# The recurrent layer's in-projections on pairs of float16 numbers, with block scales measured on the chip

## The chip, the cores and the metric

The kernel runs on one core of a Trainium2 chip. The metric is device time in microseconds of one execution. A TensorE matmul takes a stationary operand (the weights, which a separate load brings into the array) and a moving one; VectorE, ScalarE and GpSimd work beside it, each with its own instruction queue that is served in order.

## The reference

One step of a two-layer trunk on 512 prompt tokens and 32 sample tokens, 544 columns together, with a model width of 1024. Layer 0 is recurrent (RWKV-7), layer 1 is differential attention. Cut to what matters here:

```
h = rmsnorm(x, norm_w)
p, qm, gate = split(h @ w_in, [4736, 4736 + 512])     # w_in: 1024 x 7296 in layer 0
y_mix, S, last_row = rwkv_mixer(p, prev_row, S0, ...)  # token shift, then a scan over time
y_mem = mem_attention(qm, mk, mv)
x = x + (concat([y_mix, y_mem]) * silu(gate)) @ w_out
```

In the mixer each of p's columns is first blended with the column of the token before; then 24 heads of width 64 run `S = S * w + (S @ -kk) (kk * a) + v k`, and `y = S r`.

## The kernel before, in words

**Blocks.** Everything is kept transposed: features on the 128 partitions, tokens along the free dimension. A block of weights is 1024 x 128, eight tiles of 128 x 128. Layer 0's in-projection has 57 such blocks: 37 for p, 4 queries of the memory attention, 16 gates. For accuracy each fp32 operand is split into a high and a low part, and a product is three matmuls (high x high, high x low, low x high). The tokens are taken in two halves of 272. So a block is 2 x 8 x 3 = 48 matmuls of 128 x 272 into a PSUM bank (`steps`, line 481; for the first four blocks `gemm`, line 461).

**Two formats.** In layer 0 before the change the parts are fp32r. `load` (line 309) brings a block in two halves of 256 KB into the rotating tiles `raw`; `split` (line 425) queues, for each half, ScalarE's copy to the high part (`whi`) and VectorE's subtraction for the low part (`wlo`). In layer 1 the parts are float16, whose range is small, so each block is scaled by a power of two. `load_pair` (line 324) brings the block into one of four buffers inside the tile `h16s`; `square_total` (line 334) squares it with an accumulator on ScalarE, in two halves; `total_spread` (line 348) sums over the partitions by two matmuls of one column each with a matrix of ones; `scales` (line 364) makes from the sum, by integer arithmetic on the bits in VectorE, a power of two and its inverse; `scaled` (line 355) multiplies the block on GpSimd; `split_scaled` (line 393) makes the high and low parts, which the profile calls `whs`. The inverse scale enters where the product is read from PSUM. `scaled_pool` (line 1814) makes the buffers and constants for it between the layers.

**The recurrent chain.** The heads are taken in 12 pairs. For each pair `rw_chain` (line 1010) runs eight chunks of 64 tokens, one after the other, and a chunk (`chunk`, line 975) is a loop over engines: TensorE multiplies with the state (`ps_c<-SB,zr`), VectorE adds (`avz`), TensorE multiplies (`ps_c<-avz,at`), ScalarE copies (`sv`), TensorE multiplies (`ps_c<-sv,bt`), VectorE makes the new state (`SB`). Between two such hops TensorE works on the next pairs' preparation and on the in-projection blocks.

**The order of the work.** From line 1649 on every engine's order is fixed as written by the program. The loop over pairs (lines 1685 to 1724) calls the hops in turn; between them it takes work by a table (`PLAN`) and single in-projection matmuls from the generator `stream` (line 1609). How many matmuls go into a gap follows from due times, with a price per matmul, `MAIN`, in us. The blocks' jobs for ScalarE and VectorE (high parts, low parts, the shift's end) go into a queue, `put_off` (line 438). `some` (line 448) is called twice per hop and takes from its front: a job of price 0 (ScalarE's) at any call, one with a price (VectorE's) only if a budget for VectorE leaves room or the queue holds more than four jobs. `until` (line 443) forces out what a block needs, at its start. `stream` loads two blocks ahead and splits one ahead.

**Before that**, `inputs` (line 504) normalises and transposes the tokens and writes `hh` and `hl`, the two parts of h; the first four layer 0 blocks (36, 12, 0, 24) are projected outside the planned order, through `weights` and `used` (lines 404 and 413).

**Evacuations.** `shifted` (line 619) copies a p block from PSUM to `raw` on ScalarE and blends it; `gate_evac` (line 1056) makes the gate's tanh; `query_evac` scales the query.

Of the kernel before, what the change touches and what calls it, by code (L numbers as in the profile page):

```python
# [9 lines left out]
F32 = mybir.dt.float32  # L10
# [8 lines left out]
P = 128  # L19
D = 1024  # L20
KT = D // P
# [22 lines left out]
STAT1, SPREAD1, POWER1, SCALE1 = (14, 27), 12, 32, (37, 41)  # L44
SPLITS2, SCALE2 = (7, 11, 13, 17), (33, 36)
# [32 lines left out]
HOP, MAIN = 0.27, 0.126  # L78
# [64 lines left out]
class Trunk:  # L143
# [190 lines left out]
    def square_total(self, rec, q):  # L334

        if q == 0:
            rec["st"] = self.sts[rec["n"] % 4]
            if rec["n"] < 3:
                rec["junk"] = self.raws[3].bitcast(BF16)[:, :, :P]
            else:  # L340
                rec["junk"] = self.wp.tile([P, KT, P], BF16, tag="wlo", name="junkw", bufs=2)[:]
        k = slice(q * KT // 2, (q + 1) * KT // 2)
        with self.nc.allow_low_precision("a bound, rounded before a power of two is taken from it"):
            self.ae.activation(rec["junk"][:, k], rec["raw"][:, k], AF.Square, accum_out=rec["st"][:, q : q + 1])
# [37 lines left out]
    def measured(self, rec):  # L382

        if "s" not in rec:
            for q in range(2):
                self.square_total(rec, q)
            ps = self.psx.tile([P, 512], F32, tag="x", name="ps_st")
            self.total_spread(rec, ps[:, 0:1], True)
            self.scales(rec)
            for q in range(2):  # L390
                self.scaled(rec, q)

    def split_scaled(self, rec):
# [4 lines left out]
        ks = [slice(q * KT // 2, (q + 1) * KT // 2) for q in range(2)]  # L398
        todo = [(lambda k=k: self.ae.copy(hi[:, k], raw[:, k]), 0.0) for k in ks]
# [77 lines left out]
    def proj(self, src, c0, evac):  # L477
        self.gemm([self.weights(src, c0)], [(self.hh, self.hl)], evac)
        self.used()
# [24 lines left out]
    def inputs(self):  # L504

        nc, a = self.nc, self.a
        with ExitStack() as ctx:
# [16 lines left out]
            self.ahead = [(a["w_mem_k"][0], 3 * P)] + [(a["rw_in"][0], j * P) for j in (36, 12, 0, 24)]  # L524
# [10 lines left out]
            self.consts_norm(parB)  # L535
            ss = p.tile([P, 7], F32, name="ss")
# [60 lines left out]
            for k in range(KT):  # L597
                h = p.tile([P, TP], F32, tag="hn", name="hn", bufs=3)
                self.ve.scalar_tensor_tensor(h[:], xT[k], self.nw[0][:, k : k + 1], pr[0][:], ALU.mult, ALU.mult)
                self.ae.copy(self.hh[:, k, :TP], h[:])  # L600
                (self.ve if k in (2, 5, 7) else nc.gpsimd).tensor_tensor(self.hl[:, k, :TP], h[:], self.hh[:, k, :TP].bitcast(F32), ALU.subtract)  # L601
                if k in (3, 6):
                    next(kv)
                if k == 1:
                    sh = [P, KT, TS]
                    hs = p.tile(sh, F32, name="hs")
                    self.ve.tensor_tensor(hs[:], xs[:], self.nw[0].unsqueeze(2).to_broadcast(sh), ALU.mult)
                    self.ve.tensor_tensor(hs[:], hs[:], pr[1][:, :TS].unsqueeze(1).to_broadcast(sh), ALU.mult)
                    self.ae.copy(self.hh[:, :, TP:], hs[:])
                    self.ve.tensor_tensor(self.hl[:, :, TP:], hs[:], self.hh[:, :, TP:].bitcast(F32), ALU.subtract)  # L610
# [8 lines left out]
    def shifted(self, j, tag, bufs, w=None):  # L619
# [4 lines left out]
        made = {}  # L624

        def evac(ps, v):
            self.ae.copy(raw[:, v.start + 1 : v.stop + 1], ps)
            if w is not None and v.start:
# [18 lines left out]
        if w is None:  # L647
            self.proj(self.a["rw_in"][0], j * P, evac)
# [426 lines left out]
    def gate(self, src, c0, g):  # L1075

        sg, _, evac = self.gate_evac(self.o1[g])
        self.proj(src, c0, evac)
        return sg

# [8 lines left out]
    def rw_finish(self, st):  # L1089
# [31 lines left out]
        self.ve.scalar_tensor_tensor(sg[:], sg[:], 0.5, bv[:], ALU.mult, ALU.mult)  # L1121
# [63 lines left out]
    def mem_block(self, i, kind, h, mh, ml, w, out, ps_pool, ps_tag):  # L1185
# [4 lines left out]
        ps = self.psg.tile([P, 512], F32, tag="g", name="ps_g")  # L1190
        for k in range(KT):
            for u, x in ((0, mh), (0, ml), (1, mh)):
# [7 lines left out]
                yield  # L1200

# [13 lines left out]

    def mem_head(self, i, h, w, cq, cg, p):

        st = {}
        it = self.mem_steps(st, i, h, p)
        for _ in range(3):  # L1220
            next(it)
        st["q"], evac = self.query_evac(p)
        self.proj(w, cq + h * P, evac)
        for _ in range(9):
            next(it)
        sg = self.gate(w, cg + h * P, 12 + h)
        st["gate"] = lambda: sg
        for _ in it:
            pass
# [267 lines left out]
    def layer0(self, mem):  # L1497
# [6 lines left out]
        with ExitStack() as ctx:  # L1504
# [40 lines left out]
            def add(pr, src, c0, make):  # L1545
                blocks.append((src, c0, make))
# [3 lines left out]
            def add_gate(pr, st, c0, n):  # L1550
                def make(wt):
                    sg, st["gate"], evac = self.gate_evac(self.sg[n % SGB])
                    yield from self.steps(wt, evac)
                add(pr, w, c0, make)

            def add_shift(pr, of, q):
# [3 lines left out]
                add(pr, w, (12 * q + of) * P, make)  # L1560

            def add_query(pr, h):
                def make(wt):
                    mems[h]["q"], evac = self.query_evac(self.ma if h % 2 else self.rb2)
                    yield from self.steps(wt, evac)
                add(pr, w, RW_PROJ + h * P, make)
# [40 lines left out]
            blocks += [b + (None,) for b in after[:2]]  # L1607

            def stream():
                raws = [self.load(*b[:2]) for b in blocks[:2]]  # L1610
                wt = self.split(raws.pop(0))
                for _ in wt[1]:
                    self.put_off(*_)
                for i, (_, _, make) in enumerate(blocks):
                    wt, todo = wt
                    self.until(todo[-1][0])
                    if i + 2 < len(blocks):
                        raws.append(self.load(*blocks[i + 2][:2]))
                    nxt = self.split(raws.pop(0)) if raws else None
                    for _ in nxt[1] if nxt else ():  # L1620
                        self.put_off(*_)
                    if make is None:
                        self.made.append(wt)
                    else:
                        yield from make(wt)
# [117 lines left out]
        with ExitStack() as ctx:  # L1743
# [45 lines left out]
            self.scaled_pool()  # L1789
# [24 lines left out]
    def scaled_pool(self):  # L1814

        nc, p = self.nc, self.h0
        self.hh, self.hl = (lambda t: (t[:, 0], t[:, 1]))(p.tile([P, 2, KT, T], F16, tag="hl", name="h16"))
# [15 lines left out]
        with nc.allow_low_precision("a bound, rounded before a power of two is taken from it"):  # L1833
            self.ae.activation(sq, self.nw[1], AF.Square, accum_out=st)
# [4 lines left out]
        self.ve.tensor_scalar(self.nwx, self.nw[1], sx, None, ALU.mult)  # L1839
# [664 lines left out]
    def run(self):  # L2504
# [15 lines left out]
        self.hh = hp.tile([P, KT, T], F32R, tag="hh", name="hh")  # L2520
# [58 lines left out]
```

## Time and profile before

| what | value |
|---|---|
| runs before, median of 3 | 1345.06 us (1344.2 to 1348.67) |
| the profiled execution | 1347.07 us |
| its span, from the first to the last instruction | 1345.4 us |
| TensorE's granted clock, mean | 0.991 |
| layer 0's in-projection matmuls | 3 x 912, fp32r, from 35 to 698 us of the span |
| out-projection of layer 0 and what follows | 700 to 800 us |
| layer 1 | about 800 us to the end |

In the profile, PE is TensorE's matmuls, PEld its weight loads, DVE VectorE, ACT ScalarE, POOL GpSimd. A row names an operation by its tiles, `out<-in`, then the shape and type, how often it occurs (x), and after a bar the busy us in all and the mean ns of one; behind a second bar stands how long the engine was idle before these operations, and for whom it waited. Nearly all operations are issued through one helper, so they all have its line, L140, and are told apart by their tiles. In the lists of waits a row reads: who waited, for whom, us in total, times, the longest. Matmuls are pipelined, so their durations overlap; their pace is read from the starts.

### The profile page before, as it was taken

The numbers are of one execution on the slowest core, as the hardware profiler recorded it, in microseconds if no ns is written. First come the engines' busy times: TensorE is split into PE (matmuls) and PEld (weight loads), VectorE is DVE, ScalarE is ACT, GpSimd is POOL, SyncE is SP. The second block draws the span as 40 slices with busy tenths as digits, with TensorE's granted clock in tenths as the row PEclk, the third lists the DMA queues.
The fourth block names the chain that finished last, engine by engine and source line by source line (L and its number), as shares of the span: only waits on it lengthen the run. The fifth ranks groups of instructions, "written<-read, shape, count | busy, mean of one in ns | idle before, by whom it ended". The sixth has DMA issues, their size and how long they took to land. (4 is left out here: it accounts for less than half of the span.)

```text
span 1345.4 us, 32382 instructions
## 1 busy us (share of the span) xinstructions
PE 1298.5 (97%) x11786; PEld 1173.1 (87%) x11786; DVE 950.1 (71%) x2490; ACT 886.1 (66%) x2411; POOL 678.8 (50%) x1141
## 2 busy tenths in 40 slices
PE   6999999999999999999999999999999999999997
PEld 6998989999999999888899999888887887888885
DVE  6767667887787787767575355666698667987756
ACT  6665677777767867765554337777676776886652
POOL 1317765577557655860021007756555655654652
PEclk9999899999999999999999999999999999999999
DMA  7643223322322232233357445787777768774741
GB/s 235 188 114 82 62 71 88 79 70 78 88 64 69 77 99 64 63 96 98 108 158 215 131 130 152 166 186 156 165 175 169 171 159 183 171 169 111 223 150 67
DMA packets 417723, 171.56 MB, mean 128 GB/s; under 512 B 195145, under 2 KB 402514, under 8 KB 417562
## 3 DMA queue, kind: packets, MB, share of 16 engines
q1 hardware_dynamic: 417418, 168.96, 48.7%
q8 instruction: 93, 1.52, 0.5%
q14 instruction: 68, 0.56, 0.1%
q10 hardware_dynamic: 144, 0.52, 0.1%
HBM read 130.84 MB, written 41.92 MB: 128 GB/s over the span
## 5 line engine op out<-in xcount | busy, mean ns | idle before, releaser
L140 PEld LDWEIGHTS <-whs 128*128 128x128 f16 x3456 | 327.3, 98 | 67.4 <-issue 4.6
L140 PE MATMUL ps_g<-h,whs 128*128 128x272 f16 x2688 | 332.4, 279 | 1.0 <-POOL whs L140 1.0
L140 PE MATMUL ps_g<-hh,wlo 128*128 128x272 f32 x912 | 277.0, 304 | 1.5 <-DVE wlo L140 1.5
L140 PE MATMUL ps_g<-hh,whi 128*128 128x272 f32 x912 | 275.7, 303 | 0.9 <-ACT hh L140 0.9
L140 PE MATMUL ps_g<-hl,whi 128*128 128x272 f32 x912 | 271.7, 298 | 0.5 <-POOL hl L601 0.5
L890 POOL TENSOR_TENSOR tm<-u,m 102x84 f32<-102x84 f32 (+23 forms) x372 | 156.0, 419 | 166.2 <-DMA m<-sc 138.2
L140 PEld LDWEIGHTS ps_g<-hh,whi 128*128 128x128 f32 x912 | 174.8, 192 | 4.4 <-ACT hh L140 1.3
L140 PEld LDWEIGHTS ps_g<-hh,wlo 128*128 128x128 f32 x912 | 174.0, 191 | 4.9 <-DVE wlo L140 2.3
L140 PEld LDWEIGHTS ps_g<-hl,whi 128*128 128x128 f32 x912 | 174.1, 191 | 2.4 <-POOL hl L601 0.7
L892 POOL TENSOR_TENSOR u<-u,tm 102x84 f32<-102x84 f32 (+23 forms) x372 | 160.6, 432 | 29.1
L140 POOL TENSOR_TENSOR whs<-h16s,whs 128x512 f16<-128x512 f32 x126 | 147.6, 1189 | 48.3 <-ACT whs L140 46.6
L140 DVE TENSOR_TENSOR wlo<-raw,whi 128x512 fp32r<-128x512 f32 x178 | 128.4, 732 | 48.2 <-ACT whi L140 47.3
L140 ACT CAST whi<-raw 128x512 fp32r<-128x512 f32 x178 | 107.0, 616 | 35.4 <-issue 19.3
L140 POOL TENSOR_SCALAR h16s<-h16s 128x512 f32<-128x512 f32 x112 | 81.6, 741 | 93.7 <-DVE h16s L140 93.7
L140 ACT CAST whs<-h16s 128x512 f16<-128x512 f32 x144 | 84.8, 618 | 34.7 <-POOL h16s L140 33.1
L140 PE MATMUL ps_g<-hl,whs 128*128 128x272 f16 x768 | 94.1, 279 | 0.9 <-POOL whs L140 0.8
L140 ACT ACTIVATE junkw<-h16s 128x512 bf16<-128x512 f32 x138 | 86.5, 627 | 5.5 <-DMA h16s<-in_df_in_dram 4.9
L140 DVE SCALAR_TENSOR_TENSOR SB<-ps_c,dl,sd 64x64 f32<-64x64 f32 x168 | 47.4, 282 | 40.9 <-PE ps_c L140 37.4
L140 PE MATMUL ps_g<-lo,whi 128*128 128x272 f32 x256 | 73.9, 289 | 0.7 <-DVE lo L140 0.7
L140 PE MATMUL ps_g<-hi,whi 128*128 128x272 f32 x256 | 73.8, 288 | 0.7 <-ACT whi L140 0.7
L140 PE MATMUL ps_g<-hi,wlo 128*128 128x272 f32 x256 | 73.6, 288 | 0.2 <-DVE wlo L140 0.2
L140 ACT COPY sv<-ps_c 64x64 f32<-64x64 f32 x192 | 39.2, 204 | 39.8 <-PE ps_c L140 37.9
(420 smaller groups left out, 2943.6 us busy)
## 6 DMA issues: line engine op xcount, KB each, us to landing
raw<-in_rw_in_dram SPq DMA_DIRECT2D x114, 256.0 KB
h16s<-in_df_in_dram SPq DMA_DIRECT2D x112, 256.0 KB
raw<-in_w_out_dram SPq DMA_DIRECT2D x32, 256.0 KB
h16s<-in_w_out_dram SPq DMA_DIRECT2D x32, 256.0 KB
ptr<-pk SPq DMA_DIRECT2D x44, 160.0 KB
aT<-ptr SPq DMA_DIRECT2D x11, 640.0 KB
scr<-sg SPq DMA_DIRECT2D x96, 68.0 KB
out_dram<-scr SPq DMA_DIRECT2D x6, 1024.0 KB
```

The lines of the kernel that those rows point to most:

```text
L140: return lambda *a, **k: self.trunk.tie(self, issue(*a, **k))
L890: nc.gpsimd.tensor_tensor(tm[:, :n, :wd], u3[:, :n, kx : kx + 1].to_broadcast(sh), m3[:, kx : kx + 1, kx + 1 :].to_broadcast(sh), ALU.mult)
L892: nc.gpsimd.tensor_tensor(u3[:, :n, kx + 1 :], u3[:, :n, kx + 1 :], tm[:, :n, :wd], ALU.add)
```

## The change

Layer 0 takes the float16 format too. `scaled_pool(0)` is called in `inputs`, and `hh`, `hl` become float16 tiles. All 57 blocks of layer 0 go through `load_pair`, `square_total`, `total_spread`, `scales` and `split_scaled`; the eight memory blocks and the out-projection of layer 0 stay in fp32r. It differs from layer 1 in this: no pass on GpSimd scales the block; instead ScalarE's copy to the high part takes the scale as a column, and VectorE's low part is `raw * s - hi` in one instruction. Of the two halves of a block's squares ScalarE does one and VectorE the other, with an accumulator (both are ScalarE's in the first four blocks). `stream` loads up to four blocks ahead, squares three ahead, spreads and scales two ahead and splits one ahead; `total_spread` comes at the 12th of a block's 48 matmuls, `scales` at the 31st (`POWER0`). The inverse scale enters in the evacuations: `shifted`'s copy becomes an ACTIVATE with a column as its scale, the gate's tanh and the query take it as well, and the gate's last factor 0.5 becomes a column. `MAIN` goes from 0.126 to 0.117.

```diff
-HOP, MAIN = 0.27, 0.126
+HOP, MAIN = 0.27, 0.117
...
+            if self.plain and self.ordered and q:
+                x = rec["raw"][:, k]
+                self.ve.scalar_tensor_tensor(rec["junk"][:, k], x, 1.0, x, ALU.mult, ALU.mult, accum_out=rec["st"][:, q : q + 1])
+            else:
+                self.ae.activation(rec["junk"][:, k], rec["raw"][:, k], AF.Square, accum_out=rec["st"][:, q : q + 1])
...
+        if self.plain:
+            s, todo = rec["s"], []
+            for k in ks:
+                todo.append((lambda k=k: self.ae.activation(hi[:, k], raw[:, k], AF.Copy, scale=s), 0.0))
+                todo.append((lambda k=k: self.ve.scalar_tensor_tensor(lo[:, k], raw[:, k], s, hi[:, k], ALU.mult, ALU.subtract), LATER))
+            return (hi, lo, rec["inv"]), todo
...
-            self.ahead = [(a["w_mem_k"][0], 3 * P)] + [(a["rw_in"][0], j * P) for j in (36, 12, 0, 24)]
+            self.ahead = [(a["w_mem_k"][0], 3 * P)] + [(a["rw_in"][0], j * P, 0) for j in (36, 12, 0, 24)]
...
         def evac(ps, v):
-            self.ae.copy(raw[:, v.start + 1 : v.stop + 1], ps)
+            self.ae.activation(raw[:, v.start + 1 : v.stop + 1], ps, AF.Copy, scale=w[2])
...
-        self.ve.scalar_tensor_tensor(sg[:], sg[:], 0.5, bv[:], ALU.mult, ALU.mult)
+        self.ve.scalar_tensor_tensor(sg[:], sg[:], st["half"], bv[:], ALU.mult, ALU.mult)
...
+                bring(range(4))
+                squares = [lambda q=q: self.square_total(recs[2], q) for q in range(2)]
+                for fn, us in zip(squares, (0.0, LATER)):
+                    self.put_off(fn, us)
+                wt, behind = self.split(recs[0]), None
                 for _ in wt[1]:
                     self.put_off(*_)
+                for i, (_, _, _, make) in enumerate(blocks):
                     wt, todo = wt
                     self.until(todo[-1][0])
+                    for fn in squares[1:]:
+                        self.until(fn)
+                    if behind:
+                        self.scales(behind)
+                    bring(j for j in range(i + 2, i + 5) if j < i + 3 or j < len(blocks) and blocks[j][2] is not None)
+                    nxt = self.split(recs[i + 1]) if i + 1 < len(blocks) else None
                     for _ in nxt[1] if nxt else ():
                         self.put_off(*_)
+                    squares = [lambda q=q, rec=paired(i + 3): self.square_total(rec, q) for q in range(2)] if paired(i + 3) else []
+                    for fn, us in zip(squares, (0.0, LATER)):
+                        self.put_off(fn, us)
+                    self.rec = behind = paired(i + 2)
...
+                        for n, _ in enumerate(make(wt)):
+                            yield
+                            if n == POWER0 and behind:
+                                self.scales(behind)
+                                behind = None
```

More of the change, by code (lines that the diff above doesn't have):

```diff
@@ L337, in square_total @@
             rec["st"] = self.sts[rec["n"] % 4]
-            if rec["n"] < 3:
+            if self.plain:
+                if rec["n"] == 8:
+                    self.junk = self.wp.tile([P, KT, P], BF16, tag="wlo", name="junkw", bufs=2)[:]
+                rec["junk"] = self.raws[(rec["n"] + 1 + rec["n"] // 4) % 4].bitcast(BF16)[:, :, :P] if rec["n"] < 8 else self.junk
+            elif rec["n"] < 3:
                 rec["junk"] = self.raws[3].bitcast(BF16)[:, :, :P]
@@ L386, in measured @@
                 self.square_total(rec, q)
-            ps = self.psx.tile([P, 512], F32, tag="x", name="ps_st")
+            pool, tag = (self.psg, "g") if self.plain else (self.psx, "x")
+            ps = pool.tile([P, 512], F32, tag=tag, name="ps_st")
             self.total_spread(rec, ps[:, 0:1], True)
             self.scales(rec)
-            for q in range(2):
+            for q in () if self.plain else range(2):
                 self.scaled(rec, q)
@@ L475, in gemm, with proj @@
             evac(out, v)
-    def proj(self, src, c0, evac):
-        self.gemm([self.weights(src, c0)], [(self.hh, self.hl)], evac)
+    def proj(self, w, evac):
+        self.gemm([w[:2]], [(self.hh, self.hl)], evac)
         self.used()
@@ L624, in shifted @@
         made = {}
+        ramp = w is None
+        if ramp:
+            w = self.weights(None, 0)
         def evac(ps, v):
-            self.ae.copy(raw[:, v.start + 1 : v.stop + 1], ps)
-            if w is not None and v.start:
+            self.ae.activation(raw[:, v.start + 1 : v.stop + 1], ps, AF.Copy, scale=w[2])
+            if not ramp and v.start:
                 self.put_off(tail)
@@ L1200, in mem_block @@
                 yield
+                n += 1
+                if n == SPREAD1 and self.rec is not None:
+                    self.total_spread(self.rec, ps[:, 480:481], False)
     def softmax(self, ps, n, p, tag, bufs):
@@ L1543, in layer0, with add @@
             blocks, each = [], [0] * NPAIR
-            def add(pr, src, c0, make):
-                blocks.append((src, c0, make))
+            def add(pr, src, c0, make, kind=None):
+                blocks.append((src, c0, kind, make))
                 if pr is not None:
@@ L1812, in layer0, with scaled_pool @@
         self.kctx.close()
-    def scaled_pool(self):
+    def scaled_pool(self, i):
         nc, p = self.nc, self.h0
+        self.plain = i == 0
         self.hh, self.hl = (lambda t: (t[:, 0], t[:, 1]))(p.tile([P, 2, KT, T], F16, tag="hl", name="h16"))
```

69 lines of the change are left out of this document (27 added, 42 removed).

## The prediction

> **What bounds the kernel now.** I read the page first (span, busy shares, costliest groups), then the busy time by stage, then the pace of single matmuls in the timeline, then the waits of the stage that the change touches, from both sides.
>
> ```profile
> span 1345.4 us, 32382 instructions
> PE 1298.5 (97%) x11786; PEld 1173.1 (87%) x11786; DVE 950.1 (71%) x2490; ACT 886.1 (66%) x2411; POOL 678.8 (50%) x1141
> ```
>
> Over the whole span TensorE (PE) looks like the only bound. The next view, the busy time by stage, is finer. Columns: start and end of the stage, its length, then busy us and instruction count of PE, PEld, DVE, ACT and POOL, granted clock, DMA share, GB/s.
>
> ```profile
> 35.00:105.00 70.00, 67.35 (x533) 64.05 (x531) 49.29 (x118) 45.59 (x110) 18.35 (x55) 1.00 0.53 155
> 105.00:150.00 45.00, 42.55 (x394) 39.68 (x393) 27.93 (x62) 26.94 (x68) 33.14 (x84) 0.92 0.29 75
> 150.00:560.00 410.00, 404.28 (x4096) 381.48 (x4095) 318.75 (x797) 300.92 (x866) 261.87 (x582) 0.99 0.28 74
> 560.00:700.00 140.00, 132.28 (x1201) 121.57 (x1200) 95.92 (x249) 79.81 (x252) 37.45 (x91) 1.00 0.35 100
> ```
>
> The four rows are the recurrent layer's in-projections. In the long one, 150 to 560, TensorE is busy 404 of 410 us: it sets the time. But VectorE is at 78% and ScalarE at 73%, and both have to answer TensorE between two hops of the recurrent chain. The waits show how near that is. First TensorE's weight loads, which wait ahead of its matmuls, then VectorE's and ScalarE's waits, all for 150 to 560 (us in total, times, longest).
>
> ```profile
> PEld ps_c L140 <- DVE avz L140: 5.6, 17, 0.9
> PEld ps_w L140 <- DVE bv L140: 2.3, 7, 0.4
> PEld ps_w L140 <- DVE t1b L140: 2.0, 10, 0.3
> DVE SB L140 <- PE ps_c L140: 42.2, 29, 2.1
> DVE at L140 <- PE ps_at L140: 16.5, 11, 1.9
> ACT sv L140 <- PE ps_c L140: 28.3, 26, 3.2
> ```
>
> TensorE waits about 10 us for VectorE, a stall at 17 of the chain's hops already; VectorE waits 59 us for TensorE in these two groups alone. So TensorE is the bound by a small lead, and VectorE's free time (410 - 318.75 = 91 us) comes in pieces of one or two us at fixed places. The timeline of VectorE shows where. The first row is one pair's first state update, the second the next pair's; the third begins a stretch that has no idle time behind any row up to the last one.
>
> ```profile
> 231.07 0.58 DVE L140 TENSOR_SCALAR SB<-ps_c,dl 64x64 f32<-64x64 f32 x2 [1.81 <-PE ps_c L140]
> 276.85 0.58 DVE L140 TENSOR_SCALAR SB<-ps_c,dl 64x64 f32<-64x64 f32 x2 [1.89 <-PE ps_c L140]
> 278.11 0.79 DVE L140 SCALAR_TENSOR_TENSOR rkv<-raw,PA,rkv 128x544 f32<-128x544 f32 x1 [0.68 <-ACT raw L140]
> ...
> 291.27 0.67 DVE L140 TENSOR_TENSOR wlo<-raw,whi 128x512 fp32r<-128x512 f32 x1
> ```
>
> A pair takes 276.85 - 231.07 = 45.8 us, and in 291.94 - 278.11 = 13.8 us of it, 30%, VectorE never rests. That share decides my number below.
>
> **Part 1: the matmuls.** The change turns the 57 in-projection blocks (48 matmuls each) from fp32r into float16 pairs. The page has three fp32r groups of 912, of which 558, 557 and 557 lie in 150 to 560; I quote the first of each. The timeline gives the pace before, and that of a float16 run of equal shape in the attention layer.
>
> ```profile
> L140 PE MATMUL ps_g<-hh,wlo 128*128 128x272 f32 x912 | 277.0, 304 | 1.5 <-DVE wlo L140 1.5
> L140 PE MATMUL ps_g<-hh,wlo 128*128 128x272 f32 x558 | 171.6, 308 | 0.4 <-DVE wlo L140 0.4
> 419.78 0.29 PE L140 MATMUL ps_g<-hh,whi 128*128 128x272 f32 x1
> ...
> 421.29 0.28 PE L140 MATMUL ps_g<-hh,whi 128*128 128x272 f32 x1
> 1063.02 2.03 PE L140 MATMUL ps_g<-h,whs 128*128 128x272 f16 x16
> 1064.89 0.19 PE L140 MATMUL ps_g<-h16s 128*128 128x1 bf16 x2
> 1064.94 0.28 PE L140 MATMUL ps_g<-h,whs 128*128 128x272 f16 x1
> ```
>
> From the first to the last fp32r row are 12 steps: 1.51 / 12 = 0.1258 us. Sixteen float16 ones take 1064.89 - 1063.02 = 1.87, so 0.1169. That is 0.0089 less; the durations of 0.29 and 0.28 are latency and don't count. 57 x 48 = 2736 matmuls give 24.4 us. New are two one-column matmuls per block that spread the squares over the partitions: 1064.94 - 1064.89 = 0.05 us, 57 times 2.9. Net 21.5 us off TensorE: 34.8 blocks (1672 / 48) of 150 to 560 give 14.9 - 1.7 = 13.2, the other 22.2 give 9.5 - 1.1 = 8.4.
>
> **Part 2: what the other engines get for it.** The rows, of this kernel's own operations of the same kind:
>
> ```profile
> L140 DVE SCALAR_TENSOR_TENSOR junk<-xt x3: 1212/1225/1226, 5.8 to 15.2; 128x1024 f32<-128x1024 f32 x3
> L140 DVE DVE_READ_ACCUMULATOR junk<-xt x3: 80/83/84, 7.0 to 16.3; 128x1 f32 x3
> L140 DVE SCALAR_TENSOR_TENSOR hn<-bv,PB,ps_r x3: 733/734/743, 27.3 to 32.9; 128x512 f32<-128x512 f32 x3
> L140 DVE TENSOR_TENSOR wlo<-raw,whi 128x512 fp32r<-128x512 f32 x70 | 49.2, 703 | 1.5 <-ACT whi L140 1.2
> L140 DVE TENSOR_SCALAR h16s<-ps_g 128x1 int32<-128x1 int32 x68 | 10.3, 152 | 11.5 <-ACT v L140 6.0 <-ACT k L140 3.7 <-ACT mq L140 1.4
> L140 DVE TENSOR_SCALAR h16s<-h16s 128x1 int32<-128x1 int32 x129 | 23.2, 180 | 4.4
> L140 ACT ACTIVATE junkw<-h16s 128x512 bf16<-128x512 f32 x138 | 86.5, 627 | 5.5 <-DMA h16s<-in_df_in_dram 4.9
> L140 ACT ACTIVATION_READ_ACCUMULATOR junkw<-h16s 128x1 bf16 x138 | 26.9, 195 | 0.0
> L140 ACT COPY raw<-ps_g 128x272 f32<-128x272 f32 x53 | 20.5, 387 | 11.1 <-PE ps_g L140 10.5
> L140 ACT ACTIVATE k<-ps_g,h16s 128x272 f32<-128x272 f32 x24 | 11.7, 487 | 13.1 <-PE ps_g L140 13.1
> ```
>
> VectorE, per block. Its half of the squares is a 128x512 with accumulator: half of 1225 is 0.61, the 512-wide row of another form is 0.73; with the read of the accumulator, which starts under the end of the operation, I take 0.70 (0.61 to 0.82). The scales are 0.152 + 2 x 0.180 = 0.51. The two low halves change from a plain subtraction (0.703) to one with a scale in a column (0.734 for that form): 0.05 each with the loss of overlap, 0.10 (0 to 0.2). Together 1.31 us (1.1 to 1.5), so 34.8 x 1.31 = 45.6 us in 150 to 560: 364 of 397 us, 92%.
>
> ScalarE, per block. Square and read 0.82; each of the two evacuations now takes its scale from a column, 487 against 387, and I count the same 0.1 for each of the two high halves: 1.22 us, 42.5 in the stage, 343 of 397, 87%.
>
> This work sits on engines that are not the bound, so what counts is how much of it reaches TensorE. The planner's queue of small jobs is served in order; it was made for two low halves and an addition per block, and now the square joins and is forced out at the next block's start if no place was found. Behind it on VectorE queue the chain's updates (avz, SB), and TensorE's next hop waits for these. In the stretch without idle time, 30% of a pair, a job added can only push the hop: 30% of 45.6 = 13.7 us given back. In the other 70% it falls into 91 - 13 = 78 us of waits for TensorE, and I count nothing; if that cover is gone, the other 31.9 us cost too. For ScalarE I also count nothing, since it has 54 us left and its hop of the chain (sv) waits 28.3 us for TensorE. In the other three stages VectorE is busy 70%, 62% and 69%; I take half the share, 15% of 22.2 x 1.31 = 29 us: 4.4.
>
> **Small edits.** The first four blocks are measured as soon as their load is issued, so ScalarE waits for a DMA there. The nearest row is the same helper at the start of the attention layer:
>
> ```profile
> L140 ACT ACTIVATE h16s<-h16s 128x512 bf16<-128x512 f32 x6 | 3.8, 626 | 7.5 <-DMA h16s<-in_df_in_dram 7.4
> ```
>
> 7.4 / 6 = 1.2 us per block, 4.9 for four (here both halves are ScalarE's); queued behind are evacuations, which three PSUM buffers cover, and ScalarE has 24 us free in 35 to 105. Between 0 and 4.9, I take 1.0. The setup of the scale constants (some eight VectorE operations of 0.18, 1.4 us) comes in the first 35 us: 0 to 1.4, I take 0.5. Loads are issued up to four blocks ahead instead of two, on a queue where the DMA share is 0.28: nothing, and if they were late the squares of a block two ahead would be late first. The new step price 0.117 deals the same steps over the same hops: nothing. Activations stored as float16 keep their instruction counts: nothing.
>
> **The sum.** -13.2 + 13.7 - 8.4 + 4.4 + 1.0 + 0.5 = -2.0 us. The profiled execution took 1347.07 us (span 1345.4); its sum is 1345.1. The median of the runs is 1345.06, 2.0 lower, so **1343.1 us**. Differences under 0.3%, 4 us, can't be told from none here.
>
> **Rivals.** They differ in one quantity: the share of VectorE's 45.6 us that TensorE feels between 150 and 560. With the rest at -2.5 the sum is zero at 15.7 / 45.6 = 34%; over 4 us faster below 26%, over 4 us slower above 43%.
>
> A, the forecast, 15 to 45% felt: 1335 to 1350. For it: the 30% stretch. Chance 0.46, of which 0.18 is faster, 0.26 same, 0.02 slower.
>
> B, VectorE becomes the second bound of the chain: half is felt, 22.8 us, and a quarter elsewhere, 7.3: -13.2 + 22.8 - 8.4 + 7.3 + 1.5 = +10, **1355**. For it: 92% busy, in order, inside a loop that waits for TensorE in turn, with stalls on avz already. Against: waits of up to 2.1 us, which can take two jobs. Chance 0.28, slower.
>
> C, the placement hides it all: -21.5 + 1.5 = -20, **1325**. For it: 78 us of idle against 45.6. Against: the stretch above. Chance 0.21, faster.
>
> D, VectorE's square runs at half rate: 1.4 us instead of 0.70 adds 24.4 us to the stage, 389 of 397; at half felt that is 35 us, and with B's other terms -13.2 + 35 - 8.4 + 7.3 + 1.5 = +22, **1367**. Against: the 1024-wide row is this very form and takes 1.2 ns per column, against 1.4 for the 512-wide one. Chance 0.03, slower. [...]
>
> E, the change doesn't do what it says, the pace stays at 0.1258 because more than the weights' type sets it: +2.9 + 13.7 + 4.4 + 1.5 = +22.5, **1368**. Against: the float16 run above, among fp32 neighbours. Chance 0.02, slower.
>
> Faster 0.18 + 0.21 = 0.39; same 0.26; slower 0.02 + 0.28 + 0.03 + 0.02 = 0.35. The range 1325 to 1362 leaves out the lower half of C (0.10) and a fifth of B with D and E (0.10): B's own price goes by how much is felt, from 43% up.
>
> **What would show it.** In the changed profile: in-projection matmuls start every 0.117 us; new VectorE squares of about 0.70 and a read of 0.08, 53 times (ScalarE does both halves of the first four blocks); VectorE near 92% of the recurrent stage; waits of ps_c for avz or SB of 20 us and more instead of 5.6; a pair still near 45.8 us. If a pair takes 44.2 and those waits stay, C holds; if it takes 47 with waits over 35 us, B. The prediction is wrong if ScalarE's wait (sv) takes VectorE's place at the head of the list, or if the difference arises after 700 us, which no step above reaches.

## The result, and the profile after

The changed kernel is slower: 1397.45 us, the median of four runs (1396.14 to 1401.87), against 1345.17 us beside it (1344.2 to 1348.67). The ratio is 1.039, with a 95% interval of 1.0359 to 1.042. The forecast was 1343 with a range up to 1362, so both the number and the range are wrong. The profiled execution is the slowest of the four, 1401.87 us, 4.4 above the median, and every figure below from the trace of the changed kernel is of that execution. Its page begins:

```profile
span 1400.1 us, 33013 instructions
PE 1292.0 (92%) x11901; PEld 1092.6 (78%) x11901; DVE 1020.2 (73%) x2779; ACT 944.9 (67%) x2535; POOL 680.8 (49%) x1142
```

TensorE is busy 6.5 us less in a span 54.7 us longer: the loss is idle time of TensorE. To see where, I cut each trace at the first state update (`SB`) of the first pair and of the last pair, in VectorE's timeline. Before:

```profile
143.57 0.58 DVE L140 TENSOR_SCALAR SB<-ps_c,dl 64x64 f32<-64x64 f32 x2 [1.96 <-PE ps_c L140]
...
648.13 0.58 DVE L140 TENSOR_SCALAR SB<-ps_c,dl 64x64 f32<-64x64 f32 x2 [2.19 <-PE ps_c L140]
```

After:

```profile
158.47 0.58 DVE L141 TENSOR_SCALAR SB<-ps_c,dl 64x64 f32<-64x64 f32 x2 [0.45 <-PE ps_c L141]
...
700.33 0.58 DVE L141 TENSOR_SCALAR SB<-ps_c,dl 64x64 f32<-64x64 f32 x2 [1.37 <-PE ps_c L141]
```

The start is 14.9 us longer (158.47 - 143.57), the eleven pair periods 37.3 us (541.9 against 504.6), and all that follows 2.5 us. So there are two losses, and none after layer 0.

**Inside a pair.** The busy time by stage, for one pair before and one after (start and end, length, then PE, PEld, DVE, ACT, POOL, the granted clock, the DMA share, GB/s):

```profile
231.07:276.85 45.78, 45.25 (x464) 42.75 (x463) 36.34 (x90) 33.82 (x98) 29.36 (x65) 1.00 0.29 77
```

```profile
253.88:303.04 49.16, 44.33 (x472) 36.79 (x471) 41.50 (x110) 37.50 (x106) 28.69 (x64) 1.00 0.28 72
```

TensorE's idle time in a pair goes from 0.53 to 4.83 us. VectorE has 5.16 us more work, which is about four blocks of 1.29; ScalarE has 3.68 us more. Neither is full: VectorE has 7.66 us of the pair left. The four stages of the prediction, after:

```profile
35.00:105.00 70.00, 61.18 (x479) 52.01 (x479) 46.29 (x118) 44.40 (x108) 12.34 (x38) 0.90 0.51 144
105.00:150.00 45.00, 41.17 (x341) 33.81 (x340) 34.77 (x95) 32.81 (x79) 30.53 (x66) 0.96 0.36 98
150.00:560.00 410.00, 369.17 (x3895) 304.84 (x3894) 334.48 (x891) 310.19 (x867) 248.99 (x563) 0.98 0.27 70
560.00:700.00 140.00, 123.57 (x1275) 100.74 (x1273) 107.57 (x293) 92.34 (x271) 57.98 (x139) 0.99 0.30 80
```

In 410 us TensorE idles 40.8 where it idled 5.7, and the same 410 us hold 201 matmuls fewer. The groups by line and form show that the single operations cost what was forecast:

```profile
L141 PE MATMUL ps_g<-h,whs 128*128 128x272 f16 x5424 | 713.3, 281 | 1.0 <-POOL whs L141 1.0
L141 DVE SCALAR_TENSOR_TENSOR whs<-h16s,whs 128x512 f16<-128x512 f32 x114 | 87.9, 775 | 10.7 <-ACT whs L141 9.3 <-issue 0.2
L141 ACT ACTIVATE whs<-h16s 128x512 f16<-128x512 f32 x114 | 79.9, 716 | 0.5
L141 ACT ACTIVATE raw<-ps_g,h16s 128x272 f32<-128x272 f32 x74 | 36.0, 487 | 25.2 <-PE ps_g L141 24.0
L141 DVE SCALAR_TENSOR_TENSOR junkw<-h16s 128x512 bf16<-128x512 f32 x49 | 34.9, 712 | 0.2
```

The square takes 0.712 us, ScalarE's high half 0.716 and its evacuation 0.487. The low half takes 0.775 over the whole run; in the stage from 150 to 560 alone, from which the 0.703 of before is, it takes 0.766. The matmuls' pace is in the timeline:

```profile
121.26 2.72 PE L141 MATMUL ps_g<-h,whs 128*128 128x272 f16 x22
123.82 0.19 PE L141 MATMUL ps_g<-h16s 128*128 128x1 bf16 x2
```

(123.82 - 121.26) / 22 = 0.1164 us. So TensorE did get its faster matmuls, and the engines their work at the expected price. What failed is what the faster matmuls are worth, and where the added work waits.

**One wait in the pair.** The lists of waits over six pairs show it (before from 231.07 to 507.5, after from 253.9 to 549.6; us in total, times, longest). Before:

```profile
DVE SB L140 <- PE ps_c L140: 30.8, 21, 1.9
...
PEld ps_c L140 <- DVE avz L140: 3.6, 12, 0.3
```

After:

```profile
DVE h16s L141 <- ACT raw L141: 12.2, 6, 2.0
PEld ps_c L141 <- DVE SB L141: 9.1, 6, 1.5
...
PE ps_c L141 <- DVE SB L141: 7.3, 6, 1.2
...
PEld ps_c L141 <- DVE avz L141: 6.9, 18, 0.6
...
DVE SB L141 <- PE ps_c L141: 6.1, 14, 0.9
```

VectorE used to wait 30.8 us for TensorE at the state update; now 6.1, and TensorE waits for the update instead. New, and VectorE's longest, is a wait of VectorE itself: the first operation of the scales (`h16s`, which reads the sum from PSUM) waits 2.0 us, once a pair, for ScalarE's evacuation (`raw`). The timelines of that place, VectorE first (start, duration, operation, idle time before it and for whom):

```profile
307.60 1.06 DVE L141 TENSOR_TENSOR zr<-nk,de 128x512 f32<-128x512 f32 x2
310.67 0.16 DVE L141 TENSOR_SCALAR h16s<-ps_g 128x1 int32<-128x1 int32 x1 [2.00 <-ACT raw L141]
310.86 0.40 DVE L141 TENSOR_SCALAR h16s<-h16s 128x1 int32<-128x1 int32 x2
311.18 0.57 DVE L141 SCALAR_TENSOR_TENSOR SB<-ps_c,dl,sd 64x64 f32<-64x64 f32 x2
```

```profile
309.41 0.61 ACT L141 ACTIVATE junkw<-h16s 128x512 bf16<-128x512 f32 x1
309.93 0.19 ACT L141 ACTIVATION_READ_ACCUMULATOR junkw<-h16s 128x1 bf16 x1
310.14 0.49 ACT L141 ACTIVATE raw<-ps_g,h16s 128x272 f32<-128x272 f32 x1
```

```profile
308.40 0.49 PE L141 MATMUL ps_c<-sv,bt 128*128 128x128 f32 x2 [0.27 <-ACT yt L141]
...
311.80 0.49 PE L141 MATMUL ps_c<-SB,zr 128*128 128x128 f32 x2 [1.22 <-DVE SB L141]
```

The state update's input was there when `ps_c<-sv,bt` ended, at about 308.9. But ahead of it in VectorE's queue stood the scales' read, which waited for an evacuation that ScalarE did after a square. So 2 us of an idle VectorE lie on the chain. The sum (column 480) and the block's product lie in the same PSUM bank.

**The start.** TensorE's, ScalarE's and the stage view's rows at the first block's spread, after:

```profile
33.90 0.16 PE L141 MATMUL ps_st<-h16s 128*128 128x1 bf16 x1 [2.34 <-ACT h16s L141]
```

```profile
33.12 0.63 ACT L141 ACTIVATE h16s<-h16s 128x512 bf16<-128x512 f32 x1 [1.57 <-DMA h16s<-in_rw_in_dram]
```

```profile
29.00:34.00 5.00, 1.72 (x15) 1.31 (x14) 4.45 (x9) 3.43 (x9) 1.16 (x1) 0.83 0.56 176
34.00:37.00 3.00, 3.00 (x15) 2.96 (x14) 1.90 (x2) 2.56 (x7) 1.24 (x2) 0.50 0.91 249
```

and the last stretch before:

```profile
34.00:37.00 3.00, 3.00 (x23) 2.63 (x23) 3.00 (x4) 3.00 (x7) 1.76 (x2) 1.00 0.84 210
```

The spreads of the first four blocks stand in TensorE's queue, the first ones among the memory blocks' matmuls, the last among in-projection matmuls, and wait for ScalarE's squares, some of which wait for their DMA. TensorE does 1.72 us of work in five, and its granted clock falls to 0.50. The list of waits of the first 60 us has both sides:

```profile
PE ps_st L141 <- ACT h16s L141: 9.5, 3, 5.8
...
ACT h16s L141 <- DMA h16s<-in_rw_in_dram: 2.8, 3, 1.6
```

ScalarE waits 2.8 us for the loads, TensorE 9.5 for ScalarE. The first in-projection matmul starts at 46.8 us instead of 35.4. The longest of the three waits, 5.8 us up to 58.98, has another source than the blocks' loads: ScalarE's last squares stood in its queue behind `ls`, which waited 3.15 us for VectorE, and VectorE had waited 3.27 us for the load of `lam`, a parameter that was there in time in the kernel before. The granted clock is about 0.50 in three stretches (32.3 to 39.1, 42.5 to 45.9 and 56.2 to 63.0 us), in which the kernel before had 1.00; TensorE is busy 5.20 + 3.40 + 4.01 = 12.6 us in them. The memory blocks' matmuls of 128x256 start every 0.214 us in the first (34.28 to 36.63, 11 steps) and every 0.118 at clock 1.00 (46.04 to 46.63, 5 steps), so by an estimate the slower pace in the three stretches costs 12.6 x (1 - 0.118 / 0.214), some 5.7 of the 14.9 us.

### The profile page after: what moved, and what is told of

Its sections match the earlier page's. It is cut to its first block, busy times and chain, and to the rows that moved or that the text cites. A ratio compares the mean times of both kernels' runs of the same rounds, so it can differ in the third digit from the quotient of the medians.

```text
span 1400.1 us, 33013 instructions
## 1 busy us (share of the span) xinstructions
PE 1292.0 (92%) x11901; PEld 1092.6 (78%) x11901; DVE 1020.2 (73%) x2779; ACT 944.9 (67%) x2535; POOL 680.8 (49%) x1142
## 3 DMA queue, kind: packets, MB, share of 16 engines
q1 hardware_dynamic: 417418, 168.96, 46.8%
## 4 chain that ended last, share of the span: by engine, by line
PE 52%; DVE 20%; ACT 12%; DMA 6%; issue 4%; POOL 4%; SPq 2%; DVEq 0%; ACTq 0%; POOLq 0%
PE ps_g L141 36%; PE ps_c L141 3%; DVE whs L141 2%; ACT sv L141 2%; PE ps_o L141 2%; SPq L141 2%; PE ps_s L141 2%; PE ps_at L141 2%; POOL h16s L141 2%; PE ps_v L141 1%; DVE h16s L141 1%; ACT whs L141 1%; DVE SB L141 1%; DVE yt L141 1%; DVE bk L141 1%
## 5 line engine op out<-in xcount | busy, mean ns | idle before, releaser
L141 PE MATMUL ps_g<-h,whs 128*128 128x272 f16 x5424 | 713.3, 281 | 1.0 <-POOL whs L141 1.0
L141 PEld LDWEIGHTS <-whs 128*128 128x128 f16 x6192 | 588.1, 99 | 133.4 <-issue 16.4
L141 POOL TENSOR_TENSOR whs<-h16s,whs 128x512 f16<-128x512 f32 x126 | 147.6, 1189 | 47.9 <-ACT whs L141 46.2
L141 ACT ACTIVATE junkw<-h16s 128x512 bf16<-128x512 f32 x187 | 117.0, 626 | 5.2 <-DMA h16s<-in_df_in_dram 3.9
L141 DVE SCALAR_TENSOR_TENSOR whs<-h16s,whs 128x512 f16<-128x512 f32 x114 | 87.9, 775 | 10.7 <-ACT whs L141 9.3
L141 ACT ACTIVATE whs<-h16s 128x512 f16<-128x512 f32 x114 | 79.9, 716 | 0.5
L141 DVE TENSOR_TENSOR wlo<-raw,whi 128x512 fp32r<-128x512 f32 x64 | 45.7, 740 | 39.9 <-ACT whi L141 39.9
L141 POOL TENSOR_TENSOR h16s<-h16s,outf 128x512 f32<-128x512 f32 x32 | 37.1, 1179 | 46.1 <-DVE outf L141 42.5
L141 ACT CAST whi<-raw 128x512 fp32r<-128x512 f32 x64 | 37.6, 618 | 32.3 <-issue 19.3
L141 ACT ACTIVATE raw<-ps_g,h16s 128x272 f32<-128x272 f32 x74 | 36.0, 487 | 25.2 <-PE ps_g L141 24.0
L141 DVE TENSOR_SCALAR h16s<-h16s 128x1 int32<-128x1 int32 (+2 forms) x262 | 46.5, 179 | 8.5
```

The costliest lines, as they stand in the source:

```text
L141: return lambda *a, **k: self.trunk.tie(self, issue(*a, **k))
```

## The experiments

Theories at the start: W, the loss in the pairs is the scales' place in VectorE's queue behind ScalarE's evacuation; L, it is the amount of work on VectorE, wherever it waits; S, the late start is the measuring of the first four blocks; C, later, TensorE's rate doesn't set a pair although TensorE is busy 404 of 410 us. All experiments but e9 and e12 were run once, so differences under some 5 us, the spread of the changed kernel's own runs, carry little weight. The columns: device time, first update of the first pair, time from there to that of the last pair, mean of the seven periods from the third pair's first update to the tenth's. All but the first are read from VectorE's timeline as above, in one execution: of after that of 1401.87 us, of e9 one of 1342.22, of e12 one of 1341.84.

| kernel | us | first update | first to last | mean pair |
|---|---|---|---|---|
| before | 1345.17 | 143.6 | 504.6 | 45.99 |
| after | 1397.45 | 158.5 | 541.9 | 49.45 |
| e1 scales at matmul 17 | 1476.13 | 161.3 | 614.7 | 58.00 |
| e2 first four blocks' scale fixed | 1384.81 | 145.9 | 539.4 | 49.32 |
| e3 squares all on ScalarE | 1397.34 | 157.0 | 538.5 | 49.37 |
| e4 planned blocks' scale fixed | 1370.09 | 157.2 | 511.3 | 46.49 |
| e5 all scales fixed | 1351.23 | 144.9 | 506.4 | 46.08 |
| e6 before, fewer matmuls | 1340.18 | 144.6 | 497.2 | 45.15 |
| e7 scales at matmul 43 | 1380.41 | 155.8 | 524.7 | 47.56 |
| e8 planner's price 0.126 | 1392.71 | 155.5 | 536.4 | 48.74 |
| e9 float16, no scaling | 1343.71 | 141.8 | 499.3 | 45.49 |
| e10 spread late | 1395.25 | 159.7 | 530.4 | 48.49 |
| e11 e7 and e3 | 1382.26 | 154.0 | 529.2 | 48.66 |
| e12 e9 at price 0.126 | 1338.85 | 142.5 | 499.0 | 45.43 |

**e1: the scales earlier.**

```diff
-POWER0 = 30
+POWER0 = 16
```

> The scales of a block come after the 17th of the 48 matmuls instead of the 31st, so ahead of the evacuation of the first half. Theory W (VectorE's scale job waits at the head of its queue for ScalarE's evacuation of the same PSUM bank, 12.2 us in six pairs, with the chain's state update behind it): that wait goes, a pair falls from 49.3 us to 47.0-47.8, the whole by 15 to 28 us. Theory L (the amount of work on VectorE, whatever its place): the work is the same, so a pair stays at 48.8-49.8 and the whole within 6 us. Theory S (the start) says nothing of it.

It went the other way, by 79 us. TensorE's timeline, then VectorE's, of one place:

```profile
305.89 0.52 PE L141 MATMUL ps_g<-h,whs 128*128 128x272 f16 x3
309.05 0.84 PE L141 MATMUL ps_g<-h,whs 128*128 128x272 f16 x3 [2.63 <-DVE h16s L141]
```

```profile
308.84 0.16 DVE L141 TENSOR_SCALAR h16s<-ps_g 128x1 int32<-128x1 int32 x1
```

TensorE's next matmul into the bank waits 2.63 us for VectorE's read of the one column beside it, and that read stands behind other work in VectorE's queue. In one pair (264.58 to 322.46) four such waits take 7.9 us of TensorE, where the mean pair is 8.6 longer than in after. By these rows and those of after, the users of this bank followed each other in the program's order, though their columns differ. So in this kernel the read could come neither before the block's matmuls into that bank (they waited 2.63 us for it) nor just after its evacuation is asked for (in after it waited 2.00 us for that). The run also shows that "earlier" was the wrong way to test W; e7 is the right one.

**e2: the first four blocks without measuring** (their scale is a constant, 1024; squares, spreads and scales of these four are left out).

```diff
+        if self.plain:
+            rec["s"], rec["inv"] = self.fixed, self.back[rec["kind"]]
         if "s" not in rec:
```

> The four blocks that are projected ahead of the planned order get a fixed scale of 1024: their squares, spreads and scales are left out. Theory S (TensorE's spread of these blocks stands in its queue ahead of other matmuls and waits for squares that wait for a DMA, 9.5 us): the first state update of the first pair comes at 144-147 us instead of 158.5, the whole is 10 to 15 us shorter, pairs stay at 49.3. Rival (the late start comes from the clock, which is at half speed around 34 to 37 us, or from the float16 activations): under 5 us.

12.6 us less than the median of after; the first update comes 12.6 us earlier (145.9 instead of 158.5), and the pairs are as after. The clock in the stretch from 34 to 37 us is full again:

```profile
34.00:37.00 3.00, 3.00 (x27) 2.64 (x25) 2.95 (x5) 2.30 (x6) 1.04 (x1) 1.00 1.01 296
```

S holds. The waits and the half clock went away together, so this run doesn't tell their shares apart.

**e3: the squares all on ScalarE.**

```diff
-            if self.plain and self.ordered and q:
+            if False:
```

> Both halves of every block's squares on ScalarE: VectorE loses 0.70 us per block, 2.8 per pair of four blocks, ScalarE gains 0.8 per block. Theory L: a pair falls by 1 to 2.5 us, to 46.8-48.3, the whole by 12 to 30 us. Theory W: the scales still wait for the evacuation and ScalarE's evacuations come later still; a pair changes by less than 0.7 us, or grows.

Nothing: 0.1 us in the time, 0.08 in a pair, though 0.712 us a block left VectorE. L in its plain form, so much felt for each us on VectorE, falls.

**e4: the planned blocks without measuring** (53 blocks scaled by a constant; their squares, spreads and scales are left out).

```diff
-                    return recs[j] if j < len(blocks) and blocks[j][2] is not None else None
+                    return None
```

(and at the load of each block, `rec["s"]` and `rec["inv"]` set to constants as in e2)

> All blocks in the planned order get a fixed scale: no squares, spreads or scales there (53 blocks); float16 parts, column scales and all else as in the change. If squares, spreads and scales carry the loss in the pairs (theories W and L both), a pair falls to 44.0-45.0 us, under the 45.9 of before, and the whole to 1335-1350 with the late start left. If the column scales on ScalarE and VectorE carry it, a pair stays above 46.5.

The late start stays (157.2), the pairs come down to 46.49, not to 44.0 to 45.0, and the whole to 1370, not 1335 to 1350: with the measuring gone, the format still brings no gain over the 45.99 of before. By itself this left two readings open, the one of the columns of scales (46.5 and more) and that TensorE's rate is not what a pair takes; e6 and e9 separate them.

**e5: e2 and e4 together**, no measuring anywhere.

> Every block of layer 0 gets a fixed scale of 1024: all squares, spreads and scales of layer 0 are left out, float16 parts and column scales stay. This is what the float16 matmuls bring without measuring. If the losses of the start (12.5 us) and of the measuring in the pairs (27 us) add up: 1384.8 - 27.2 = 1357 us. Theory C (the chain's hops, not TensorE's rate, set the pair, so 0.0089 us per matmul buys nothing there): at or above 1343, pairs 45.5 where the clock is undisturbed, as without the change. Theory K (TensorE's rate counts, and half clock, seen in five places of the run with the planned blocks fixed, hid it): pairs of 44.2 where the clock is full.

1351.23, 6 us under the 1357 of the sum, which is about what single runs can tell; the pairs, 46.08, are nearer to C's 45.5 than to K's 44.2. Measuring costs 46.2 us of the 52.3; what is left, float16 with scales from columns, is 6 us slower than before.

**e6: the kernel before with fewer matmuls.** Of each planned block 4 of 48 matmuls are left out (their products are missing from the sum), 212 x 0.126 = 26.7 us of TensorE's work, with their weight loads, and nothing else changes.

```diff
-                    self.te.matmul(ps[:, :TH], w[t][:, k, :], x[:, k, v], start=k == 0 and x is self.hh and t == 0,
-                                             stop=k == KT - 1 and t == 1)
+                    if t == 0 or k not in (1, 5) or not self.hh.dtype == F32R:
+                        self.te.matmul(ps[:, :TH], w[t][:, k, :], x[:, k, v], start=k == 0 and x is self.hh and t == 0,
+                                                 stop=k == KT - 1 and t == 1)
```

> The kernel before, with 4 of the 48 matmuls of each in-projection block in the planned order left out (the low weights of two of the eight tiles, in both halves), so part of the product is missing; their places in the order stay. This takes 4 x 0.126 = 0.50 us per block off TensorE, 2.0 per pair of four blocks, and nothing off or on any other engine. If TensorE's rate sets the pair: pairs fall from 45.7 to 43.7, the whole by 20 to 27 us. Theory C (the chain through VectorE and ScalarE sets it): pairs at 45.0 or more, the whole by under 10 us.

1340.18 against 1345.00 beside it: 4.8 us for 26.7, and 0.8 in a pair for 2.0. The stage from 150 to 560:

```profile
150.00:560.00 410.00, 394.78 (x3995) 370.21 (x3993) 326.00 (x810) 304.49 (x877) 264.48 (x589) 0.98 0.29 75
```

TensorE's idle time goes from 5.7 to 15.2 us: most of the time set free is not used. C holds: TensorE's lead over the chain was about 0.8 us a pair. Rival C of the prediction (1325, all added work hidden) needed the full 21.5 us from the faster matmuls, and they were not to be had.

**e7: the scales later**, after the 43rd matmul, when the first half's evacuation is long done.

```diff
-POWER0 = 30
+POWER0 = 42
```

> The scales come after the 43rd of the 48 matmuls instead of the 31st, by when ScalarE has evacuated the bank. Theory W: the wait of VectorE's scale job for ScalarE (2.0 us, once in a pair) goes below 0.5 and pairs fall from 49.3 to 47.3-48.3. If the wait only moves to another place or the sum of the work counts: 48.8 or more.

1380.41: 17.0 us less than the median of after. From the first update to the last it is 17.2 us (524.7 against 541.9). The row of the scales' read, over the whole run, after and then e7:

```profile
L141 DVE TENSOR_SCALAR h16s<-ps_g 128x1 int32<-128x1 int32 x121 | 18.3, 151 | 31.0 <-ACT raw L141 16.0 <-ACT v L141 6.0 <-ACT k L141 3.7
```

```profile
L141 DVE TENSOR_SCALAR h16s<-ps_g 128x1 int32<-128x1 int32 x121 | 18.3, 151 | 12.4 <-ACT v L141 6.0 <-ACT k L141 3.7 <-ACT mq L141 1.4
```

The 16.0 us of idle VectorE for `raw` are gone, and the pairs are shorter by about as much. The same instructions, one group of them later: W holds.

**e8: the planner's price back.**

```diff
-HOP, MAIN = 0.27, 0.117
+HOP, MAIN = 0.27, 0.126
```

> The change with the planner's price of a matmul back at 0.126. If the price only deals the same steps over the same hops, as the prediction had it: pairs within 0.3 us of 49.3 and the whole within 4 us of the change. If the new price put jobs or matmuls at worse places: pairs shorter by 0.5 us or more.

1392.71, 4.7 us less, at the edge of what one run can tell, with pairs shorter by 0.7 us. It isn't the price alone: over six pairs (249 to 542) the wait of `h16s` for `raw` is 5.9 us here, where after has 12.2. With the matmuls dealt otherwise, the same wait is half as long, so this gain and that of e7 are in part the same.

**e9 and e12: float16 alone.** Float16 parts with no scaling at all: no squares, spreads, scales; copies and subtractions as before. Such a kernel loses digits of small weights, so it is an experiment and no replacement. e12 is e9 with `MAIN` at 0.126.

```diff
-                todo.append((lambda k=k: self.ae.activation(hi[:, k], raw[:, k], AF.Copy, scale=s), 0.0))
-                todo.append((lambda k=k: self.ve.scalar_tensor_tensor(lo[:, k], raw[:, k], s, hi[:, k], ALU.mult, ALU.subtract), LATER))
+                todo.append((lambda k=k: self.ae.copy(hi[:, k], raw[:, k]), 0.0))
+                todo.append((lambda k=k: self.ve.tensor_tensor(lo[:, k], raw[:, k], hi[:, k], ALU.subtract), LATER))
...
-            self.ae.activation(raw[:, v.start + 1 : v.stop + 1], ps, AF.Copy, scale=w[2])
+            self.ae.copy(raw[:, v.start + 1 : v.stop + 1], ps)
```

> Float16 parts of layer 0's in-projections without any scaling: the squares, spreads, scales and the columns of scales are left out, in h too; high parts, low parts and evacuations are the plain copies and subtractions of the kernel before, with float16 outputs. So the matmuls' type alone is changed (low parts of small weights lose digits). The run with fewer matmuls gave pairs of 44.8 for 2.0 us taken off TensorE; here 1.7 are taken off. Theory C (TensorE's time is felt to two fifths): pairs of 44.9-45.2, the whole 1336-1341. Theory F (float16 also costs something beyond its columns of scales, for example in the low parts): pairs of 45.5, the whole at 1343-1347. Theory K (TensorE's rate counts in full): 44.2 and 1325.

> As the run without scaling (the same parts are left out), with the planner's price at 0.126 instead of 0.117. From the change itself this price took 0.4 us per pair. If the new price is bad of itself: 3 to 5 us below the run without scaling. If it only interacted with the squares' places: within 2 us of it.

e9: 1343.71 (ten runs), ratio 0.9996 with an interval of 0.9973 to 1.002, no difference. e12: 1338.85 (four runs, the profiled one the slowest), ratio 0.9948 with 0.9931 to 0.9964, half a per cent below the kernel before. So the whole gain of the format, loads up to four blocks ahead included, is 1.9 us at the new price and 6.7 at the old, and by the medians the price costs 4.9. Where these arise the traces don't show: the pairs take 45.49 and 45.43. e9 lies in the range of F; e12 lies in that of C by its time and still in that of F by its pairs. So K is out, and a small cost of the float16 format beyond its columns is not. One pair of e9:

```profile
276.35:321.36 45.01, 43.07 (x464) 36.58 (x463) 36.71 (x91) 33.81 (x98) 29.64 (x67) 1.00 0.30 78
```

TensorE has 2.18 us less to do than in the pair of before, and the pair is 0.77 shorter.

**e10: the spread after the 28th matmul, the scales at the next block's start.**

```diff
-POWER0 = 30
+POWER0 = 999
+SPREAD0 = 28
...
-                    if n == SPREAD1 and self.rec is not None:
+                    if n == (SPREAD0 if self.plain else SPREAD1) and self.rec is not None:
```

> The change with the spread after the 28th matmul of a block (in the bank of its second half) and the scales at the next block's start, so that TensorE waits later for the squares (0.8 us once per pair) and VectorE not for the first evacuation. Theory W+: below the 47.5 us pairs of the run with late scales, 46.5 to 47.0. If the wait moves to the evacuation of the second half, at the block's start: 47.5 or more.

W+ did not come: 1395.25, with pairs of 48.49. Its list of waits over six pairs (247 to 540):

```profile
PEld ps_c L142 <- DVE avz L142: 11.0, 7, 1.8
ACT whs L142 <- DVE h16s L142: 10.4, 6, 1.7
...
PE ps_c L142 <- DVE avz L142: 9.7, 6, 1.6
PE ps_at L142 <- DVE bk L142: 6.5, 6, 1.2
```

VectorE's read still waits for the evacuation, 4.6 us in these pairs, as the second alternative had it. And the scales now come so late that ScalarE's high halves wait for them, and the chain stalls at another update, `avz`. A better place for one wait can't be reasoned from that wait alone.

**e11: e7 and e3 together.**

```diff
-POWER0 = 30
+POWER0 = 42
...
-            if self.plain and self.ordered and q:
+            if False:
```

> Late scales (after the 43rd matmul), and all squares on ScalarE. With the wait gone, theory L (VectorE's work of 2.8 us per pair is felt) expects pairs of 45.8-46.8 instead of 47.5. If the two engines' loads weigh alike (what VectorE loses ScalarE gains): 47.2-47.8.

1382.26, no gain over e7; the pairs, 48.66, are 1.1 us longer than there and above both ranges. 0.71 us a block moved from VectorE to ScalarE is worth nothing with the wait, and costs something without it.

## Why the prediction was wrong, step by step

**The unit costs were right.** Square 0.712 (forecast 0.70), low halves 0.063 more in the stage from 150 to 560 (0.05), ScalarE's evacuation and high half 0.1 more, the pace 0.1164 (0.1169); VectorE's added work is 1.29 us a block (1.31). So rival E is out, and rival D too, which had 1.4 us for the square. What failed is how these pieces were laid on the path.

**First failing step: "TensorE is busy 404 of 410 us: it sets the time".** From it came -13.2 and -8.4, the largest terms. e6 takes 26.7 us off TensorE alone and gets 4.8 back; e9 takes off 24, by the pace, and gets 1.9, e12 6.7. TensorE was full because the program spreads a pair's in-projection matmuls over the gaps of the recurrent chain; a full engine does not show that a shorter matmul shortens the gap. By e6 a gap shrank by less than half of what TensorE was spared (0.8 of 2.0 us in a pair), and then the chain's hops on the other engines held it. My own rows hinted at it: TensorE's 10 us of waits for VectorE, with a stall at 17 of the chain's hops. I wrote "by a small lead" and then counted as if the lead were large. In place of -21.6 stands -2 to -7.

**Second: the share of added work that is felt.** I took 30% of a pair, the stretch in which VectorE never rests, and 13.7 us for the long stage. The pairs grew by 37.3 us from first to last; with the measuring out (e5) 35.5 of them are gone. 17.2 of those go with one wait (e7), in which VectorE does nothing: about half of the cost is not VectorE's busy time but the place of the scales' read in the queue. My sum had no such term, since each job was priced by its duration. Yet a row I quoted carried it: layer 1's `h16s<-ps_g` has 11.5 us of idle before it, for `v`, `k` and `mq`, ScalarE's evacuations. I used its 152 ns and not its wait. The other 18.3 us are the rest of the squares, spreads and scales, beside a chain with little slack on either engine (e3, e11: squares moved to ScalarE gain nothing). One piece is in the trace of after: TensorE's spread (`ps_g<-h16s`) waits 4.1 us in six pairs for VectorE's square, 0.7 once a pair. How the others divide was not tried.

**Third: the start, 1.0 + 0.5.** Measured 14.9 by the trace, 12.6 by e2. The bound of 4.9 was on ScalarE's wait for its DMA, with evacuations behind it, and that wait is inside it, 2.8. But TensorE's spreads wait for ScalarE, in order, with other matmuls behind them, 9.5 us, and the granted clock falls to half, some 5.7 us more by the estimate above. I named what was queued behind ScalarE's instruction, not what was behind TensorE's, nor what stood ahead of ScalarE's (the 3.15 us for `ls`).

**Fourth: edits costed at nothing.** The planner's price costs about 5 us by the times (e8, and e9 against e12). It deals the same number of matmuls in other shares over the gaps; in e8 this halves the scales' wait, and for e12 it stays open where the time is won. Scales from columns cost 7.1 us in the pairs (e5 against e9, first to last, one execution each); I had 0.10 us a block for them on VectorE, 30% felt, and ScalarE's 0.4 at nothing.

**What held.** Rival B came nearest, with a chain that ends on VectorE as often as on TensorE; but it asked for pairs of 47 and 1355, where they take 49.45 and the whole 1397, and its price went by the amount of VectorE's work, which e3 contradicts. TensorE's waits for VectorE at SB and avz are there as forecast (PEld's 12.6 + 9.0 us between 150 and 560, forecast 20 and more). In the six pairs TensorE's list is led by SB and avz, not by `sv` (2.0 us over the six pairs), and nothing arises behind the recurrent layer (2.5 us). VectorE's 92% did not come: 82% of the stage, because the stage grew instead.

**The account**, by the times: the measuring 46.2 (after to e5), scaling with its columns 7.5 (e5 to e9), the price 4.9 (e9 to e12), against a gain of 6.7 from the rest of the change (e12 against the kernel before): 51.9 for a difference of 52.3. These are steps of one ladder, so that they add up proves nothing. What can be held against something is inside the measuring: start 12.6 (e2) and planned blocks 27.4 (e4) make 40.0, and e5 has 46.2 for both; the 6 us between are about the noise of single runs. The scales' wait, 17.2 (e7), is the largest single cause that was isolated in the pairs.

What stays open: that users of one bank wait for each other though their columns differ was seen in both directions (2.63 us of TensorE for VectorE's read in e1, 2.00 of VectorE for ScalarE's evacuation in after, gone in e7), but why is not shown, and the sum in a bank of its own was not tried. A version with the measuring that beats the kernel before was not found: e2 and e7 together would take off about 30 of 52 us, by their sum, which was not run.

## What to carry to other kernels

Where a program fills one engine's gaps from a list, that engine's busy share alone does not show what sets the time: take a twelfth of its matmuls away, as in e6, before counting on a faster operation. Price an added operation by what it waits for and what stands behind it in its queue, not by its duration; a row's idle column, in the kernel's own uses of the same helper, can show that wait beforehand. A value that several engines read needs a moment at which nobody else has claims on its place (e7, 17.2 us from the first update to the last); whether a place of its own does the same was not tried.

## What the runs showed of the hardware that was not expected

- TensorE's granted clock fell to 0.50 at idle gaps of different length, and once with hardly any idle time ahead. In after it is 0.50 from 32.3 us on, 0.7 us into a gap of 2.34 (from 31.56), with 1.84 us of idle time in the 12.3 us ahead; from 42.5 on, 0.4 us behind a gap of 1.40; and from 56.2 on, 3.0 us into one of 5.76. In the kernel before it falls at 309.8 us after 7.8 us with 0.07 us of idle time, as the stage view shows.

```profile
302.00:309.80 7.80, 7.73 (x89) 7.33 (x88) 5.12 (x15) 6.16 (x18) 1.91 (x5) 1.00 0.31 81
309.80:313.20 3.40, 3.40 (x17) 3.40 (x16) 3.03 (x10) 2.37 (x9) 2.89 (x7) 0.50 0.57 164
```

  So these traces give no rule for it. Whether the fall is the cause of some of the lost time in the pairs, or only follows the waits, was not separated; e1, with the most waits, has the lowest mean clock, 0.96 against 0.983.
- A scale from a column isn't free on either engine. ScalarE's 128x272 evacuation takes 486 ns with one in after and 387 without in the kernel before (150 to 560). Its 128x512 float16 high half takes 716 with one, and 618 as a plain copy in layer 1 (both in after, the whole run). VectorE's 128x512 low half takes 766 with one in after and 715 without in e9 (150 to 560).
- Float16 weights load in 99 ns where fp32r ones took 191 (mean of a load in the groups by line), and PEld's busy time in a pair falls from 42.75 to 36.79 us. How much of it is felt as time was not separated from the shorter matmuls; both together gave 1.9 us in e9.
